# Convolution taps of the delta heads read PSUM accumulators: two bank pairs instead of padded SBUF rows

## The chip, the core and the metric

The kernel runs on one core of a Trainium2 chip. The metric is the device time of one execution in microseconds (us). The engines are written as the profile writes them: PE is TensorE's matrix multiplication and PEld its weight load, DVE is VectorE, ACT is ScalarE, POOL is GpSimd and SP is SyncE, which here issues the DMA transfers. Numbers such as L314 are lines of the kernel, as printed below.

## The reference, cut to what matters

Two blocks follow one another on a sequence of 1024 positions with 1024 features in float32. The first block projects the normalised input and has two kinds of heads: neighbourhood attention (8 heads of 64) and the gated delta rule (4 heads of 128). Before the delta rule, the projected q, k and v of the delta heads pass through a convolution of five taps, each channel by itself, centred, with zeros beyond both ends of the sequence, and then through SiLU:

```
def _centred_depthwise_conv(x, w):
    return lax.conv_general_dilated(x, w[:, None, :], window_strides=(1,),
        padding=[(DN_CONV // 2, DN_CONV // 2)],
        dimension_numbers=('NWC', 'WIO', 'NWC'), feature_group_count=c)
...
h = _rmsnorm(x, norm_w)
proj = jnp.einsum('bld,de->ble', h, w_in)
aq, ak, av, az, dq, dk, dv, dz, b_f, a_f, b_b, a_b = _split_proj(proj)
...
qkv = jax.nn.silu(_centred_depthwise_conv(jnp.concatenate([dq, dk, dv], axis=-1), conv_w))
dq, dk, dv = jnp.split(qkv, 3, axis=-1)
dq, dk, dv = _l2norm(to_bhld(dq)), _l2norm(to_bhld(dk)), to_bhld(dv)
...
o_f = _gated_delta_chunked(dq, dk, dv, g_f, beta_f)
o_b = flip(_gated_delta_chunked(flip(dq), flip(dk), flip(dv), flip(g_b), flip(beta_b)))
```

So there are 3 x 4 = 12 convolutions of a row block of 128 channels by 1024 positions. The gates (b, a) give decays between positions of a chunk, and each delta chunk needs a triangular solve. The second block (stick-breaking attention and retention) has a wider projection and takes most of the time; nothing in it is edited.

## The kernel before, in words

**Stages.** By the profile's clock the first block's preparation (load, norm, transposes into hT, the projection of the gates) lasts to about 57 us. The four delta heads follow, to about 230 us. Then come the projections of the neighbourhood attention (called na_proj here: products at L102 and L112, column blocks of 384 and 512), to about 302 us, while DVE and POOL still finish the last delta head. From there to about 460 us the neighbourhood attention (na) runs together with the triangular solver. The rest, to 2250 us, is the delta recurrence, the output projection and the second block. The delta rule's solver (L457 and L459, updates of X from the chunk matrices N in DRAM) works on all heads at once and so begins after the last head.

**Projection.** A product in float32 is made in three passes of a high and a low half (h1hi, h1lo with wu). Function dense_col makes one column block transposed, 128 channels by 1024 positions, as 48 matmuls of 128x512 at L112 into two PSUM accumulators; dense_tok makes 128 positions by n columns at L102. The weights come by DMA to raw, and POOL splits them into the halves (L70, L71) of wu.

**PSUM before.** There are two pools for the whole program: acc has three banks (each 128x512), z two, and t, o and p one each. They are never reopened.

**One delta head.** For each of q, k, v (index b): dense_col; two copies on ACT from the accumulators into a padded SBUF row pad of 1028 columns (L309), whose four edge columns POOL sets to zero (L306 and the line behind it); then on DVE the first tap as a product (L312) and four more taps that read pad shifted and add to cv (L314); then SiLU on ACT (L317). There are two buffers of pad and two of cv. From the results come rq (the norm of q, L324 and L325), the transposed and normalised k (kt, L335 to L340, through a z bank), kT (L349), v (vt), and for each direction the decays E (L379), the chunk matrices N (L400, from bank t), the matrices IT (L415, from bank p) and the scaled copies sct (L424, L428), which go to DRAM (d_N, d_pk, d_v). N and IT share two buffers with the tag IN; sct and vt share two.

**The gate chain.** Ahead of the heads, graw (the log decays) is summed along the positions by two matmuls (L279, L280) into a z bank, copied to gc (L281), transposed (L283), copied to growt (L285) and sent to DRAM (d_g).

**Order.** Each engine executes its instructions in a fixed order, which the framework's scheduler works out at build time from the dependencies and its own estimates. A pool's memory is reused only when everything that used it before has ended. So an edit of one place may move instructions of all engines around it.

## Time and profile before

| | before |
|---|---|
| median of 3 runs | 2250.59 us (2245.22 to 2253.38) |
| the profiled execution | 2252.17 us |
| its span, first to last instruction | 2250.5 us |
| mean granted TensorE clock | 0.984 |
| busy: PE, DVE, ACT, POOL | 2163.0, 1102.5, 766.0, 1105.4 us |

The profile is of one execution. Its time lies 1.6 us above the median and 1.7 us above its span. Busy times are those of whole instructions; a share of the clock of 1 is full speed. In a timeline a row has the start, the length, the engine, the line, the operation, output<-inputs, the shape and, in brackets, the idle time before it with what ended that idle time.

### The profile page before, as it was taken

Reading aid. Unit: us, or ns where it says so; the run is one execution under the profiler, and the core shown is the slowest. Engines: PE = TensorE matmul, PEld = TensorE weight load, DVE = VectorE, ACT = ScalarE, POOL = GpSimd, SP = SyncE. Lnnn points to the kernel's source line nnn. Section 1 sums busy time; section 2 is a strip of 40 time slices with the busy share of each in tenths; the row PEclk is TensorE's granted clock in tenths of the full one; section 3 lists DMA queues with packets and bytes.
Section 4 is the critical chain, followed back from the end, with each engine's and each line's share of the span. In section 5 each row is a group of like instructions: output and inputs, shape, how many; then the busy total and the mean of one; then the engine's idle time right before and its main releaser. Section 6 shows DMA issues by size and latency. Waiting matters only on the chain.

```text
span 2250.5 us, 33410 instructions
## 1 busy us (share of the span) xinstructions
PE 2163.0 (96%) x12325; PEld 1882.8 (84%) x12325; DVE 1102.5 (49%) x1980; ACT 766.0 (34%) x1912; POOL 1105.4 (49%) x1451
## 2 busy tenths in 40 slices
PE   7999888899999999999999999999999999999999
PEld 7777777787889878999999998888988888878887
DVE  4688879953446553566555655123333432231321
ACT  5354433445555322444333433112222322321200
POOL 6667777773101345344333334356565755354532
PEclk9999999899999999999999999999999999999999
DMA  4255740126377542111111112212333323564433
GB/s 132 83 152 157 206 129 26 36 82 190 90 278 246 176 130 63 41 61 57 57 42 34 43 57 71 89 58 79 107 94 120 126 92 114 179 227 159 146 109 106
DMA packets 240196, 250.27 MB, mean 111 GB/s; under 512 B 40161, under 2 KB 175521, under 8 KB 239777
## 3 DMA queue, kind: packets, MB, share of 16 engines
q1 hardware_dynamic: 240032, 248.14, 35.3%
q8 instruction: 97, 1.59, 0.3%
q14 instruction: 67, 0.54, 0.1%
HBM read 172.56 MB, written 75.53 MB: 110 GB/s over the span
## 4 chain that ended last, share of the span: by engine, by line
PE 68%; DVE 11%; POOL 6%; issue 5%; DMA 5%; ACT 2%; SPq 1%; POOLq 0%; DVEq 0%; ACTq 0%
PE acc L112 29%; PE acc L102 17%; PE acc L853 3%; PE po L1083 2%; PE pz L1051 2%; DVE X L459 2%; DVE svt L457 2%; POOL wu L71 2%; DVE cv L314 1%; POOL wu L70 1%; DMA raw<-in_w_in_dram 1%; PE pz L546 1%; PE pt L563 1%; POOL ss L126 1%; PE pp L577 1%
## 5 line engine op out<-in xcount | busy, mean ns | idle before, releaser
L112 PE MATMUL acc<-h2h,wu 128*128 128x512 f32 x1440 | 438.4, 393 | 0.7 <-ACT lg L958 0.7
L102 PE MATMUL acc<-wu,h2h 128*128 128x384 f32 (+1 forms) x1536 | 366.8, 322 | 6.6 <-ACT lg L972 2.2
L71 POOL TENSOR_TENSOR wu<-raw,wu 128x512 fp32r<-128x512 f32 (+3 forms) x276 | 366.3, 1335 | 7.2
L70 POOL TENSOR_SCALAR wu<-raw 128x512 fp32r<-128x512 f32 (+3 forms) x276 | 205.8, 749 | 313.0 <-PE acc L112 202.4
L112 PEld LDWEIGHTS acc<-h2h,wu 128*128 128x128 f32 x1440 | 269.5, 188 | 54.9 <-ACT lg L958 1.1
L102 PEld LDWEIGHTS acc<-wu,h2h 128*128 128x128 f32 x1536 | 265.8, 191 | 11.6 <-ACT lg L972 2.6
L112 PE MATMUL acc<-h2l,wu 128*128 128x512 f32 x720 | 265.2, 392 | 0.0
L102 PE MATMUL acc<-wu,h2l 128*128 128x384 f32 (+1 forms) x768 | 244.9, 321 | 0.0
L102 PE MATMUL acc<-wu,h1hi 128*128 128x384 f32 (+2 forms) x768 | 192.2, 334 | 11.1 <-DVE kS L512 5.2
L112 PE MATMUL acc<-h1hi,wu 128*128 128x512 f32 x512 | 167.3, 416 | 6.8 <-ACT pad L309 3.2
L125 POOL TENSOR_SCALAR ss<-ss 128x2 f32<-128x2 f32 (+2 forms) x136 | 36.7, 270 | 269.6 <-ACT sq L1001 215.0
L112 PEld LDWEIGHTS acc<-h2l,wu 128*128 128x128 f32 x720 | 135.0, 188 | 26.5
L102 PEld LDWEIGHTS acc<-wu,h1hi 128*128 128x128 f32 x768 | 137.0, 195 | 16.0 <-issue 6.5
L102 PEld LDWEIGHTS acc<-wu,h2l 128*128 128x128 f32 x768 | 146.1, 191 | 1.6
L112 PEld LDWEIGHTS acc<-h1hi,wu 128*128 128x128 f32 x512 | 100.4, 198 | 31.8 <-ACT pad L309 4.2
L102 PE MATMUL acc<-wu,h1lo 128*128 128x384 f32 (+2 forms) x384 | 126.7, 333 | 0.0
L126 POOL TENSOR_TENSOR ss<-ss,mhalf 128x2 f32<-128x2 f32 (+2 forms) x136 | 118.9, 875 | 8.3
L112 PE MATMUL acc<-h1lo,wu 128*128 128x512 f32 x256 | 97.9, 411 | 0.0
L1001 ACT ACTIVATE sq<-acc 128x128 f32<-128x128 f32 x128 | 35.5, 286 | 138.7 <-PE acc L102 125.8
L314 DVE SCALAR_TENSOR_TENSOR cv<-pad,c_conv_w,cv 128x1024 f32<-128x1024 f32 x48 | 76.6, 1596 | 1.1
L112 PE MATMUL acc<-oah,wu 128*128 128x512 f32 x256 | 76.1, 393 | 1.0 <-DVE sg L1275 0.6
L102 PEld LDWEIGHTS acc<-wu,h1lo 128*128 128x128 f32 x384 | 74.8, 195 | 0.4 <-issue 0.2
(553 smaller groups left out, 4438.1 us busy)
## 6 DMA issues: line engine op xcount, KB each, us to landing
raw<-in_w_in_dram SPq DMA_DIRECT2D x192, 256.0 KB, 3.0
d_pk<-sct SPq DMA_DIRECT2D x24, 512.0 KB, 4.3
raw<-in_w_out_dram SPq DMA_DIRECT2D x40, 256.0 KB, 3.0
wsa<-d_pk SPq DMA_DIRECT2D x16, 512.0 KB, 6.4
wsb<-d_pk SPq DMA_DIRECT2D x16, 512.0 KB, 7.4
d_sg<-lg SPq DMA_DIRECT2D x32, 256.0 KB, 2.4
sg<-d_sg SPq DMA_DIRECT2D x32, 256.0 KB, 3.4
raw<-in_w_in_dram SPq DMA_DIRECT2D x32, 192.0 KB, 2.8
```

Of the source, the lines that this page charges most:

```text
L70: nc.gpsimd.tensor_scalar(out=u[:, 0, :], in0=raw, scalar1=1.0, scalar2=0.0, op0=ALU.mult, op1=ALU.add)
L71: nc.gpsimd.tensor_tensor(out=u[:, 1, :], in0=raw, in1=f32(u[:, 0, :]), op=ALU.subtract)
L102: nc.tensor.matmul(acc[:, :n], lhsT=hT[a][:, k, m * P:(m + 1) * P], rhs=us[k][:, b, c0:c0 + n], start=(k == 0 and i == 0), stop=(k == NK - ...
L112: nc.tensor.matmul(accs[half], lhsT=us[k][:, b, c0:c0 + P], rhs=hT[a][:, k, half * 512:(half + 1) * 512], start=(k == 0 and i == 0), stop= ...
L125: nc.gpsimd.tensor_scalar(out=dst, in0=src, scalar1=mul, scalar2=eps, op0=ALU.mult, op1=ALU.add)
L126: nc.gpsimd.tensor_tensor(out=dst, in0=dst, in1=mhalf[:, :eshape], op=ALU.pow)
L314: nc.vector.scalar_tensor_tensor(out=cv, in0=pad[:, i:i + T], scalar=conv_w[:, blk, i:i + 1], in1=cv, op0=ALU.mult, op1=ALU.add)
L457: eng.tensor_tensor(out=tv, in0=X[:, a:a + n, j:j + 1].to_broadcast([P, n, w]), in1=X[:, j:j + 1, j + 1:64].to_broadcast([P, n, w]), op=AL ...
L459: eng.tensor_tensor(out=X[:, a:a + n, j + 1:64], in0=X[:, a:a + n, j + 1:64], in1=tv, op=ALU.add)
L853: nc.tensor.matmul(acc, lhsT=us[k][:, y, (b % 4) * P:(b % 4 + 1) * P], rhs=token_set(mT[x][:, k, 0:T], s), start=(k == 0 and i == 0), stop ...
L1051: nc.tensor.matmul(pz[:, :w], lhsT=qk[0][a][:, i * P:(i + 1) * P], rhs=qk[1][b][:, c0:c0 + w], start=(x == 0), stop=(x == 2))
L1083: nc.tensor.matmul(po[:, i0 * P:512], lhsT=v[a][:, c0 // P + kb, :], rhs=wT[b][:, :n], start=(diag and kb == 0 and x == 0), stop=(diag == ...
```

## The change

The PSUM pools are now opened and closed by a helper, banks(layout). Up to the heads and after them the layout is that of before (three accumulators a, two z banks, t, o, p). For the four delta heads it is two pairs c of two adjacent banks each, one z bank, t, o and p. All PSUM pools close and open at each switch. The projection of a delta block goes into a pair, so that its 1024 columns are contiguous. ACT makes the centre tap from the pair with a scale per channel and writes cv; DVE adds the four other taps, which read the pair shifted, over 1023 or 1022 columns, so that no padded row and no zeroed edges are needed. cv and sct (with vt) get three buffers instead of two, IN four instead of two.

```
-    psA = ctx.enter_context(tc.tile_pool(name="psA", bufs=3, space=PSUM))
-    psB = ctx.enter_context(tc.tile_pool(name="psB", bufs=1, space=PSUM))
+    def banks(layout):
+        while ps_pools:
+            ps_pools.pop().__exit__(None, None, None)
+        ps.clear()
+        for i, (tags, bufs) in enumerate(layout):
+            p_ = tc.tile_pool(name="ps" + tags, bufs=bufs, space=PSUM)
+            ps_pools.append(p_)
+            pl = p_.__enter__()
+            for t_ in tags:
+                ps[t_] = pl
+    banks((("a", 3), ("ztop", 1)))
...
+    banks((("c", 2), ("ztop", 1)))
     for h in range(4):
-        vt = dn.tile([P, NM, P], F32, tag="sct", name="vt", bufs=2)
+        vt = dn.tile([P, NM, P], F32, tag="sct", name="vt", bufs=3)
...
-            pad = dc.tile([P, T + 4], F32, tag="pad", name="pad", bufs=2)
-            nc.gpsimd.memset(pad[:, 0:2], 0.0)
-            nc.gpsimd.memset(pad[:, T + 2:T + 4], 0.0)
-            for half, acc in enumerate(dense_col(hT, us, b * P)):
-                nc.scalar.copy(out=pad[:, 2 + half * 512:2 + half * 512 + 512], in_=acc)
-            cv = dc.tile([P, T], F32, tag="cv", name="cv", bufs=2)
-            nc.vector.tensor_scalar_mul(out=cv, in0=pad[:, 0:T], scalar1=conv_w[:, blk, 0:1])
-            for i in range(1, 5):
-                nc.vector.scalar_tensor_tensor(out=cv, in0=pad[:, i:i + T], scalar=conv_w[:, blk, i:i + 1],
-                                               in1=cv, op0=ALU.mult, op1=ALU.add)
+            acc = pair()
+            dense_col(hT, us, b * P, acc)
+            cv = dc.tile([P, T], F32, tag="cv", name="cv", bufs=3)
+            for half in range(2):
+                hs = slice(half * 512, half * 512 + 512)
+                nc.scalar.activation(out=cv[:, hs], in_=acc[:, hs], func=AF.Copy, scale=conv_w[:, blk, 2:3])
+            for i in (1, 3, 0, 4):
+                a_, b_ = max(0, 2 - i), min(T, T + 2 - i)
+                nc.vector.scalar_tensor_tensor(out=cv[:, a_:b_], in0=acc[:, a_ + i - 2:b_ + i - 2], scalar=conv_w[:, blk, i:i + 1],
+                                               in1=cv[:, a_:b_], op0=ALU.mult, op1=ALU.add)
...
-                        N = dn.tile([P, 4, P], F32, tag="IN", name="N", bufs=2)
+                        N = dn.tile([P, 4, P], F32, tag="IN", name="N", bufs=4)
...
+    banks((("a", 3), ("ztop", 1)))
     naB = tc.tile_pool(name="naB", bufs=1, side="right")
```

In the changed kernel the lines lie 17 to 19 further down: L102 is L119, L112 is L129, L279 and L280 are L296 and L297, L283 is L300, the taps of L314 are L332, E of L379 is L397, N of L400 is L418, IT of L415 is L433, sct of L424 and L428 is L442 and L446. The order of all engines is the same again from about 635 us on.

**Where the heads begin.** PE before, from the last products ahead of the gate sums (L279, L280) on; those ahead are products of the first delta block, of which there are 37 ahead of the sums:

```order
L112 MATMUL acc<-h1lo_99,wu 128x512
L112 MATMUL acc<-h1hi_98,wu 128x512 x3
L112 MATMUL acc<-h1lo_99,wu 128x512 x2
L112 MATMUL acc<-h1hi_98,wu 128x512 x3
L279 MATMUL pz<-graw,trile 128x32
L280 MATMUL pz<-graw,trige 128x32
L112 MATMUL acc<-h1hi_98,wu 128x512
L112 MATMUL acc<-h1lo_99,wu 128x512 x2
L112 MATMUL acc<-h1hi_98,wu 128x512 x4
```

and in the changed kernel, where L119 is the projection of the gates, L296, L297 and L300 the gate chain, and L129 the first products into a pair:

```order
L119 MATMUL acc<-wu,h1lo_99 128x272
L119 MATMUL acc<-wu,h1hi_98 128x272 x2
L119 MATMUL acc<-wu,h1lo_99 128x272
L296 MATMUL pz<-graw,trile 128x32
L297 MATMUL pz<-graw,trige 128x32
L300 MATMUL pz<-ident,gc 64x128
L129 MATMUL pair<-h1hi_96,wu 128x512 x2
L129 MATMUL pair<-h1lo_97,wu 128x512 x2
```

The products of the first delta block stood ahead of the gate sums and now stand behind them and behind the transpose of gc.

**Where the heads end.** PE before: the last product of the twelfth delta block (L112) and the first products of na_proj (L102):

```order
L112 MATMUL acc<-h1hi_98,wu 128x512 x4
L112 MATMUL acc<-h1lo_99,wu 128x512 x2
L112 MATMUL acc<-h1hi_98,wu 128x512 x2
L102 MATMUL acc<-wu,h1hi_96 128x384 x2
L102 MATMUL acc<-wu,h1lo_97 128x384
L102 MATMUL acc<-wu,h1hi_96 128x384 x2
```

and in the changed kernel, with pair products (L129), the last head's chunk products (L414, L429), the sums for rq (L342), the transposes of k (L353), and then na_proj (L119):

```order
L129 MATMUL pair<-h1hi_98,wu 128x512 x4
L129 MATMUL pair<-h1lo_99,wu 128x512 x2
L129 MATMUL pair<-h1hi_98,wu 128x512 x2
L414 MATMUL pt<-kT 128x128 x4
L342 MATMUL pz<-ones_79,sq 128x2 x8
L353 MATMUL pz<-ident,s 128x128 x4
L429 MATMUL pp<-s,kT 128x128 x4
L119 MATMUL acc<-wu,h1hi_96 128x384 x2
L119 MATMUL acc<-wu,h1lo_97 128x384
L119 MATMUL acc<-wu,h1hi_96 128x384 x2
```

The first product of na_proj now writes a bank of a reopened pool, and waits in this order for the last tap of the twelfth convolution, which reads a pair in the same memory.

**The twelfth convolution on DVE.** Before, from its first tap (L312) to the last (L314), with IT (L415) and sct (L428) of the head before among them:

```order
L312 TENSOR_SCALAR cv<-pad,c_conv_w 128x1024
L415 TENSOR_TENSOR IT<-pp,E 128x512
L314 SCALAR_TENSOR_TENSOR cv<-pad,c_conv_w,cv 128x1024
L415 TENSOR_TENSOR IT<-pp,E 128x512
L314 SCALAR_TENSOR_TENSOR cv<-pad,c_conv_w,cv 128x1024 x2
L428 TENSOR_TENSOR sct<-kt,el 128x1024
L314 SCALAR_TENSOR_TENSOR cv<-pad,c_conv_w,cv 128x1024
L415 TENSOR_TENSOR IT<-pp,E 128x512
```

and in the changed kernel, its four taps at L332, with E (L397), rq (L343), el (L386, L391), sct (L442, L446) and IT (L433) among them:

```order
L332 SCALAR_TENSOR_TENSOR cv<-pair,c_conv_w,cv 128x1023
L397 TENSOR_TENSOR E<-G,gc 128x1024
L332 SCALAR_TENSOR_TENSOR cv<-pair,c_conv_w,cv 128x1023
L343 COPY rq<-pz 128x8
L386 TENSOR_TENSOR el<-G,gc 128x8
L442 TENSOR_TENSOR sct<-kT,G 128x1024
L446 TENSOR_TENSOR sct<-kt,el 128x1024
L332 SCALAR_TENSOR_TENSOR cv<-pair,c_conv_w,cv 128x1022
L433 TENSOR_TENSOR IT<-pp,E 128x512
L391 TENSOR_TENSOR el<-el,beta 128x8
L332 SCALAR_TENSOR_TENSOR cv<-pair,c_conv_w,cv 128x1022
```

Before, the five taps had two IT, one sct and one more IT behind; now the four taps have an E, two sct, one IT and small operations among them.

## Rows read from the trace of the kernel before

**Rows 1.** Stretches: length, busy PE, PEld, DVE, ACT, POOL, clock, DMA share, GB/s.

```profile
60.00:230.00 170.00, 159.28 (x759) 129.43 (x757) 137.47 (x121) 74.33 (x136) 117.25 (x109) 0.96 0.49 132
230.00:300.00 70.00, 57.14 (x308) 52.38 (x308) 50.25 (x75) 25.80 (x72) 49.48 (x50) 0.92 0.78 200
300.00:460.00 160.00, 142.23 (x836) 119.36 (x835) 150.03 (x331) 64.15 (x176) 128.48 (x182) 0.93 0.14 44
460.00:2250.00 1790.00, 1756.68 (x10126) 1538.34 (x10124) 740.06 (x1399) 568.23 (x1463) 772.38 (x1051) 0.99 0.34 111
```

**Rows 2.** Timeline of PE around the gate sums.

```profile
45.11 0.39 PE L112 MATMUL acc<-h1hi,wu 128*128 128x512 f32 x1
...
53.00 0.87 PE L112 MATMUL acc<-h1hi,wu 128*128 128x512 f32 x3
56.71 0.64 PE L279 MATMUL pz<-graw,trile 128*128 128x32 f32 x2 [2.84 <-DVE graw L275]
```

**Rows 3.** Timeline of DVE around the gate sums.

```profile
57.81 0.22 DVE L281 COPY gc<-pz 128x64 f32<-128x64 f32 x1 [1.16 <-PE pz L280]
65.08 0.28 DVE L285 COPY growt<-pz 64x128 f32<-64x128 f32 x1 [7.04 <-PE pz L283]
```

**Rows 4.** Busy time as in rows 1, of the stretch behind the gate sums.

```profile
55.00:65.00 10.00, 8.29 (x26) 6.70 (x27) 1.85 (x3) 0.00 (x0) 4.45 (x6) 0.66 0.57 164
```

**Rows 5.** Groups of DVE, 57 to 300 us: busy, mean ns | idle before, releasers.

```profile
L314 DVE SCALAR_TENSOR_TENSOR cv<-pad,c_conv_w,cv 128x1024 f32<-128x1024 f32 x48 | 76.6, 1596 | 1.1
L424 DVE TENSOR_TENSOR sct<-kT,G 128x1024 f32<-128x1024 f32 x8 | 14.3, 1785 | 4.3 <-POOL E L380 2.2 <-ACT kT L350 2.1
L428 DVE TENSOR_TENSOR sct<-kt,el 128x1024 f32<-128x1024 f32 x8 | 12.8, 1597 | 5.8 <-DMA d_pk<-sct 5.8
L312 DVE TENSOR_SCALAR cv<-pad,c_conv_w 128x1024 f32<-128x1024 f32 x12 | 11.7, 974 | 5.8 <-ACT pad L309 5.8
L379 DVE TENSOR_TENSOR E<-G,gc 128x1024 f32<-128x1024 f32 x8 | 11.4, 1423 | 0.0
L415 DVE TENSOR_TENSOR IT<-pp,E 128x512 f32<-128x512 f32 x16 | 10.7, 679 | 1.4 <-DMA d_pk<-IT 1.4
```

**Rows 6.** Lines L314, L400, L309: ns min/median/max; for L314 who waited (us, times).

```profile
L314 DVE SCALAR_TENSOR_TENSOR cv<-pad,c_conv_w,cv x48: 1269/1431/3252, 69.3 to 244.5; 128x1024 f32<-128x1024 f32 x48
...
  ACT s L317: 35.2, 8
  POOL pad L306: 12.7, 4
...
L400 DVE SCALAR_TENSOR_TENSOR N<-pt,E x16: 674/680/692, 117.2 to 275.2; 128x512 f32<-128x512 f32 x16
...
L309 ACT COPY pad<-acc x24: 566/588/596, 67.3 to 232.9; 128x512 f32<-128x512 f32 x24
```

**Rows 7.** Waits of PE, 40 to 300 us: total, times, longest.

```profile
PE po L349 <- DVE kt L340: 4.9, 4, 3.3
PE acc L508 <- DVE kn L500: 4.2, 3, 3.1
PE acc L112 <- ACT pad L309: 3.2, 3, 2.1
```

**Rows 8.** Timeline of PE at the end of the heads and of na_proj.

```profile
226.91 0.62 PE L112 MATMUL acc<-h1hi,wu 128*128 128x512 f32 x2
...
232.96 0.61 PE L102 MATMUL acc<-wu,h1hi 128*128 128x384 f32 x2 [2.79 <-ACT pad L309]
...
302.44 0.38 PE L531 MATMUL po<-ident,qd 128*128 128x128 f32 x2
```

**Rows 9.** Timeline of DVE: last tap, last N, first update of the solver.

```profile
244.46 1.62 DVE L314 SCALAR_TENSOR_TENSOR cv<-pad,c_conv_w,cv 128x1024 f32<-128x1024 f32 x1
...
274.35 1.50 DVE L400 SCALAR_TENSOR_TENSOR N<-pt,E 128x512 f32<-128x512 f32 x2
...
295.08 0.25 DVE L457 TENSOR_TENSOR svt<-X 128x54 f32<-128x54 f32 x1 [2.97 <-DMA X<-d_N]
```

More of the change, by code (lines that the diff above doesn't have):

```diff
@@ L47, in tile_kernel @@
     wpool = ctx.enter_context(tc.tile_pool(name="wpool", bufs=10))
-    psA = ctx.enter_context(tc.tile_pool(name="psA", bufs=3, space=PSUM))
-    psB = ctx.enter_context(tc.tile_pool(name="psB", bufs=1, space=PSUM))
+    ps = {}
+    ps_pools = []
+    def banks(layout):
[9 more added lines that the diff above has]
+    banks((("a", 3), ("ztop", 1)))
+    ctx.callback(banks, ())
     dram = ctx.enter_context(tc.tile_pool(name="dram", bufs=1, space=DRAM))
@@ L88, in bank, with pair @@
         if tag == "a":
-            return psA.tile([P, w], F32, tag="a", name="acc")
-        return psB.tile([P, w], F32, tag=tag, name="p" + tag, bufs=2 if tag == "z" else 1)
+            return ps["a"].tile([P, w], F32, tag="a", name="acc")
+        return ps[tag].tile([P, w], F32, tag=tag, name="p" + tag, bufs=2 if tag == "z" and "a" in ps else 1)
+    def pair():
+        return ps["c"].tile([P, T], F32, tag="c", name="pair")
     def dense_tok(hT, us, c0, n, order=None):
@@ L105, in dense_tok, with dense_col @@
                 yield m, a
-    def dense_col(hT, us, c0):
-        accs = [bank("a") for _ in range(2)]
+    def dense_col(hT, us, c0, acc2=None):
+        accs = [bank("a") for _ in range(2)] if acc2 is None else [acc2[:, 0:512], acc2[:, 512:1024]]
         for k in range(NK):
@@ L422, in tile_kernel @@
             for f, src in enumerate((kT, sT[0])):
-                sc_t = dn.tile([P, NM, P], F32, tag="sct", name="sct", bufs=2)
+                sc_t = dn.tile([P, NM, P], F32, tag="sct", name="sct", bufs=3)
                 (nc.gpsimd if f else nc.vector).tensor_tensor(out=sc_t.rearrange("p n c -> p (n c)"), in0=src, in1=G.rearrange("p n c -> p (n c)"),
@@ L426, in tile_kernel @@
                 nc.sync.dma_start(out=d_pk[d, :, :, f, h, :].rearrange("n p c -> p n c"), in_=sc_t)
-            sc_t = dn.tile([P, NM, P], F32, tag="sct", name="sct", bufs=2)
+            sc_t = dn.tile([P, NM, P], F32, tag="sct", name="sct", bufs=3)
             nc.vector.tensor_tensor(out=sc_t, in0=kt, in1=el[:, dh, :].unsqueeze(2).to_broadcast([P, NM, P]), op=ALU.mult)
```

4 lines of the change are left out of this document (2 added, 2 removed).

## The prediction

> **What bounds the kernel now.** The busy time in four stretches comes first [rows 1]. From 460 us on PE is busy for 1756.7 of 1790 us at a granted clock of 0.99. Nothing there is edited, so this stretch only moves as a whole. What the change can win or lose lies before 460 us. There PE sits idle for 170 - 159.3 = 10.7 us in the heads, 70 - 57.1 = 12.9 us in na_proj and 160 - 142.2 = 17.8 us in na. Where PE runs, its clock lies below full speed: (1 - clock) x length gives 6.8, 5.6 and 11.2 us. So about 65 us in all is not PE at its peak, and this is the pot.
>
> Next, who keeps PE waiting. DVE is busy for 137.5 of 170 us in the heads and for 150 of 160 us in na [rows 1]. PE's largest waits up to 300 us end with DVE's kt, DVE's kn and ACT's copies to pad [rows 7]. The copies in turn stand in ACT's queue behind SiLU, which waited 35.2 us in 8 cases for the last tap, and POOL waited 12.7 us to clear a pad [rows 6]. So in the heads PE and DVE are near each other, and DVE is what runs late: PE's last product of the twelfth delta block starts at 226.91 us [rows 8], and the last tap on it ends at 244.46 + 1.62 = 246.1 us [rows 9], 18.7 us behind the product's end at 227.4. At the far end the solver can't begin before the last N (274.35 us on) has gone to DRAM and come back as X: its first update is at 295.08 us [rows 9], 7 us before PE ends na_proj at 302.4 [rows 8]. From there DVE, with its 150 of 160 us, sets na.
>
> **The change, part by part.** The sum is made against the profiled execution, 2252.2 us; the median is 1.6 us lower.
>
> Opening switch. Before, 37 products of the first delta block ran from 45.11 us to 53.00 + 0.87 = 53.9 us, and the gate sums followed at 56.71 us, 2.84 us after them [rows 2]. These products gave PE work while ACT and DVE made graw. Now the pair pool opens only when all PSUM tiles of the preparation are done with, the last being the one that growt is copied from; the order shows all pair products behind the gate chain. That chain can't move forward, since graw doesn't. So the first pair product comes after the sums (56.71 + about 1.1), the copy of gc (57.81 + 0.22 [rows 3]), a transpose and the copy of growt (0.28 [rows 3]): about 59 us. 37 products of 8.8 / 37 = 0.237 us must be made up, 8.8 us, and PE reaches its 38th place some 1.4 us later by the chain: **+10**. The low clock behind the sums (0.66 [rows 4]) was there before and stays; bounds +8.8 to +14, the upper one if it lasts over those 37 too. What the earlier growt gives (65.08 before [rows 3], about 58.5 now) is that the decays E come early; DVE has nothing else then, so this counts in the next term.
>
> Heads. DVE loses 12 first taps of 0.974 us, 11.7 us [rows 5]. The other 48 took 1.596 us on average [rows 5], 1.269 at best and 3.252 at worst [rows 6]. No row shows a tap that reads PSUM over 1024 columns. The nearest is N, the same operation with one input in PSUM over 512 columns: 674 to 692 ns [rows 6], twice which is 1.36; the fastest tap from SBUF bounds it at 1.27. I take 1.30, as one long operation should lie under two short ones: 48 x 0.296 = 14.2 us. No gain at all is the other bound. So DVE has 25.9 us less of its 137.5. The centre tap on ACT takes the place of the copy (0.588 us [rows 6], 24 of both); even 0.1 us more each is hidden, since ACT is busy for 74 of 170 us [rows 1]. Were it not, 2.4 us is its whole cost. POOL's 24 clears and its wait of 12.7 us go; more buffers of sct and IN can take away DVE's waits of 5.8 and 1.4 us for DMA [rows 5]. A head then needs on DVE 12 x 1.30 (taps) + 3 x 1.42 (E) + 2 x 1.42 (E by beta, priced as E) + 10 x 0.68 (N, IT, kt) + 3.6 + 3.2 (sct) = 36 us and some small ones [rows 5, 6], about 38, where it was about 44; PE needs some 40: a quarter of the 182.3 us from 45.11 to 227.4 less 2.84, 10.7 and 6.8 of waits and low clock. PE becomes the slower of the two. Of its 10.7 idle and 6.8 clock I let 11.5 go: **-11.5**, bounds 0 and -17.5.
>
> Against it stands that less is held between product and taps. Before, two pads and the accumulators let PE end the product of block i+2 while the taps of block i ran; now block i+2 needs the pair of block i, free only after its fourth tap. Late taps up to one block's products (48 x 0.237 = 11.4 us) stay hidden, later ones stop PE. One z bank instead of two also puts the second half of k's transposes behind kt of the first.
>
> The Trainium skill ("Perfetto Trace Analysis", section Optimizing Scalar/DVE Operations) gives DVE about 60 ns of access overhead per instruction on SBUF and about 125 ns on PSUM. By that, as an estimate, 48 taps would save 3.1 us less, and the sum would be at most that much higher. No run here shows that difference by itself; N's rows contain whatever it is.
>
> Closing switch. Before, na_proj followed the last L112 product without a wait, and the first copy to pad stopped it later for 2.79 us [rows 8]. Now the order puts its first product behind the twelfth block's last tap. After PE's last pair product come on ACT two centre taps of 0.588 [rows 6], on DVE four taps of 1.30 with an E of 1.42, two sct of 1.79 and 1.60 and an IT of 0.68 between them [rows 5], and about 1 us of small ones and hand-overs: 13.3 us. Against that PE has 20 small products, some 2.5 us. So it idles 10.8 us, some 2.5 us go by the lower clock after it, and the old 2.79 us are gone: **+10.7**, bounds +8 (E and sct done sooner) and +20 (the old lag of 18.7 us and its clock).
>
> Rest of na_proj. DVE is some 7 us further there and na_proj's copies compete with less of the last head: I halve its 10.1 us of other idle time and 5.6 of clock: **-7.5**, bounds 0 and -15.7.
>
> Na. PE's last pair product should end near 226 us (227.4 + 10 - 11.5), so the last tap at 239 instead of 246. From there to the last N the order has two E, two E by beta, two kt, two IT, two sct and four N: 17 us [rows 5, 6], where it took 246.1 to 275.9. N is done about 16 us earlier, and X may start at about 279 us, while PE ends na_proj at 302.4 + 10 - 11.5 + 10.7 - 7.5 = 304. So DVE enters na with up to 18 us of solver behind it. But the order uses this: eight more updates stand ahead of the first reduction of na's scores, about 10 us. What stays is **-8**, bounds 0 and -19, of 29 us idle and clock there.
>
> Sum: +10 - 11.5 + 10.7 - 7.5 - 8 = -6.3 on 2252.2, 2245.9 us, and against the median **2244**.
>
> **Rivals.** (A) The sum as it stands: two new waits cost about what the faster heads and the earlier solver give. 2238 to 2253.
>
> (B) The early solver pays in full: DVE is busy for 150 of 160 us in na [rows 1], which speaks for it; the order, which puts updates ahead of the scores again, against. -19 instead of -8, and the closing at its lower bound: about 2230, 2224 to 2237.
>
> (C) The pair is held too long, slower. If E, sct and kt between the taps, with their own waits on POOL and ACT, keep the taps more than 11.4 us behind the products, PE stops at each pair. Speaking for it: DVE was 18.7 us late before; against: 38 us of DVE to 40 of PE per head. 2.5 us at each of the last nine pairs are 22 us: 2266, 2257 to 2275. It decides from about 2 us a pair on. The Trainium skill ("PSUM — Partial Sum Buffer", section Summary: rules for kernel authors) says to evacuate promptly because PSUM is tight; by that rule this case would come true. The trace of before shows banks evacuated by short copies and PE still waiting for them [rows 7], so it doesn't settle it.
>
> (D) The taps from PSUM take the 1.6 us of those from SBUF, so that only 11.7 of 25.9 us come: the heads give -5, closing costs 1.2 more, na gives -4: about 2256, 2250 to 2260. N's steady 0.68 speaks against it.
>
> **How the numbers follow.** A 0.42, B 0.25, C 0.20, D 0.13. A measurement of this kernel tells 0.5%, 11.3 us, from no change: below 2239.3 is faster, above 2261.8 slower. Faster is B and the edge of A, 0.31; slower most of C, 0.18; the rest 0.51. The range 2229 to 2264 leaves out the lower end of B (0.09) and the upper part of C (0.11). A's own range is 2238 to 2253.
>
> **What would show it.** Opening: PE without a product from about 45 to 59 us. Heads: L332 at 1.27 to 1.36 us, hardly spread; PE idle under 5 us from 65 us on, last pair product ending near 226 us. Closing: PE's wait ended by the last tap, 9 to 13 us. Last N near 260 us, the solver's first update near 279, na_proj's end near 304. The prediction is wrong if PE waits for taps within the heads (C), or if what stands at 460 us before comes more than 15 us earlier (B).

## The result, and the profile after

The changed kernel takes 2265.23 us (median of 5 runs, 2262.35 to 2266.81) against 2250.59 us for the kernel before in the same session. The ratio is 1.0078 [1.0062, 1.0093]: slower by 0.78%, 15 us by the medians, where no clear change was forecast, and 1 us above the range's upper end. The profiled execution has a span of 2265.1 us at a clock of 0.981.

The four stretches, as in [rows 1]:

```profile
60.00:230.00 170.00, 161.63 (x784) 132.83 (x784) 105.04 (x106) 69.13 (x131) 84.93 (x86) 0.98 0.49 132
230.00:300.00 70.00, 51.11 (x282) 48.91 (x282) 51.24 (x72) 29.80 (x75) 43.98 (x48) 0.82 0.84 220
300.00:460.00 160.00, 136.94 (x800) 115.82 (x799) 150.40 (x326) 59.75 (x159) 133.28 (x186) 0.93 0.13 41
460.00:2250.00 1790.00, 1758.60 (x10153) 1540.33 (x10154) 747.66 (x1405) 572.15 (x1477) 773.71 (x1050) 0.99 0.34 110
```

DVE's busy time in the heads fell from 137.5 to 105.0 us, and PE's idle time there from 10.7 to 8.4 us. What is worse lies behind: PE is idle for 18.9 us in na_proj's stretch, at a clock of 0.82, and for 23.1 us in na's.

PE at the opening, which answers to [rows 2] and [rows 3]:

```profile
57.65 0.61 PE L296 MATMUL pz<-graw,trile 128*128 128x32 f32 x2 [11.41 <-POOL wu L85]
58.07 0.61 PE L297 MATMUL pz<-graw,trige 128*128 128x32 f32 x2
59.00 0.42 PE L300 MATMUL pz<-ident,gc 128*64 128x128 f32 x1 [0.32 <-DVE gc L298]
59.89 1.19 PE L129 MATMUL pair<-h1hi,wu 128*128 128x512 f32 x2 [0.47 <-DVE growt L302]
```

PE stands from about 46 us (the gates' projection ends 1 us later than before) and begins with the first pair at 59.89 us, where "about 59" was forecast. (The row puts the 11.41 us down to POOL's wu; what the sums read is graw, which DVE ends at 57.55 us.)

The DVE groups, as in [rows 5], and who waited for the centre tap (L329) and for the taps (L332), as in [rows 6]:

```profile
L332 DVE SCALAR_TENSOR_TENSOR cv<-pair,c_conv_w,cv 128x1023 f32<-128x1023 f32 x24 | 30.7, 1280 | 22.5 <-ACT cv L329 22.2
L332 DVE SCALAR_TENSOR_TENSOR cv<-pair,c_conv_w,cv 128x1022 f32<-128x1022 f32 x24 | 30.6, 1276 | 0.3
```

```profile
L332 DVE SCALAR_TENSOR_TENSOR cv<-pair,c_conv_w,cv x48: 1265/1282/1285, 74.0 to 248.1; 128x1023 f32<-128x1023 f32 x24, 128x1022 f32<-128x1022 f32 x24
...
  ACT cv L329: 22.2, 7
...
  ACT s L335: 26.8, 7
...
L329 ACT ACTIVATE cv<-pair,c_conv_w x24: 670/685/707, 72.7 to 232.3; 128x512 f32<-128x512 f32 x24
```

A tap from PSUM takes 1.265 to 1.285 us, with hardly a spread. DVE sat idle for 22.2 us, in 7 cases, until ACT had made the centre tap. But 17.9 us of these lie in the first four convolutions, where ACT itself waits for PE's product and makes the centre tap at once; DVE only keeps PE's pace there. The second convolution, on ACT and on DVE:

```profile
83.86 1.27 ACT L329 ACTIVATE cv<-pair,c_conv_w 128x512 f32<-128x512 f32 x2 [2.17 <-PE pair L129]
```

```profile
85.16 5.24 DVE L332 SCALAR_TENSOR_TENSOR cv<-pair,c_conv_w,cv 128x1023 f32<-128x1023 f32 x4 [5.90 <-ACT cv L329]
```

PE and DVE at the end of the heads and of na_proj, which answer to [rows 8] and [rows 9]:

```profile
228.59 0.64 PE L129 MATMUL pair<-h1hi,wu 128*128 128x512 f32 x2
...
233.95 3.57 PE L342 MATMUL pz<-ones,sq 128*128 128x2 f32 x16 [3.84 <-ACT sq L339]
238.49 1.11 PE L353 MATMUL pz<-ident,s 128*128 128x128 f32 x4 [0.96 <-DVE rq L343]
248.15 2.08 PE L429 MATMUL pp<-s,kT 128*128 128x128 f32 x8 [8.55 <-DVE IT L433]
249.88 0.99 PE L119 MATMUL acc<-wu,h1hi 128*128 128x384 f32 x2
```

```profile
248.09 1.27 DVE L332 SCALAR_TENSOR_TENSOR cv<-pair,c_conv_w,cv 128x1022 f32<-128x1022 f32 x1
...
271.57 1.27 DVE L418 SCALAR_TENSOR_TENSOR N<-pt,E 128x512 f32<-128x512 f32 x2
...
292.06 0.25 DVE L476 TENSOR_TENSOR svt<-X 128x54 f32<-128x54 f32 x1 [7.38 <-DMA X<-d_N]
```

The last pair product ends at 229.2 us, 1.7 us later than before. The last tap ends at 249.4 us, 20.2 us behind the product, and 0.5 us later comes na_proj's first product, at 249.88 instead of 227.37. (The profile puts PE's wait of 8.55 us down to IT, since the chunk products L429 stand ahead of na_proj in the queue and needed the bank that IT read; the last tap ended 1.3 us later still.) With na_proj's and na's products of L102 and L119 matched by their count, the lateness is 17.8 us at 253, 8.3 us at 270, 10.9 us at 307, 14.3 us at 447 and 14.6 us at the end. The last N ends at 272.8 us and the solver starts at 292.06, 3 us earlier than before [rows 9], where 16 were forecast.

### The profile page after: what moved, and what is told of

The parts are those of the page before. It is cut to its first block, busy times and chain, and to the rows that moved or that the text cites. A ratio compares the mean times of both kernels' runs of the same rounds, so it can differ in the third digit from the quotient of the medians.

```text
span 2265.1 us, 33370 instructions
## 1 busy us (share of the span) xinstructions
PE 2157.4 (95%) x12325; PEld 1882.7 (83%) x12325; DVE 1081.9 (48%) x1968; ACT 765.7 (34%) x1910; POOL 1073.3 (47%) x1427
## 4 chain that ended last, share of the span: by engine, by line
PE 70%; DVE 9%; POOL 7%; issue 5%; DMA 5%; ACT 2%; SPq 0%; POOLq 0%; ACTq 0%; DVEq 0%
PE acc L129 29%; PE acc L119 17%; PE pair L129 3%; PE acc L872 3%; PE po L1102 2%; PE pz L1070 2%; DVE X L478 2%; POOL wu L85 2%; DVE svt L476 2%; POOL wu L84 1%; DMA raw<-in_w_in_dram 1%; PE pz L565 1%; POOL ss L143 1%; PE pt L1223 1%; PE pt L1097 1%
## 5 line engine op out<-in xcount | busy, mean ns | idle before, releaser
L129 PE MATMUL acc<-h2h,wu 128*128 128x512 f32 x1440 | 438.1, 392 | 0.4 <-ACT lg L977 0.4
L119 PE MATMUL acc<-wu,h2h 128*128 128x384 f32 (+1 forms) x1536 | 366.6, 322 | 6.4 <-DVE sq L1026 2.0
L85 POOL TENSOR_TENSOR wu<-raw,wu 128x512 fp32r<-128x512 f32 (+3 forms) x276 | 352.4, 1285 | 8.5
L84 POOL TENSOR_SCALAR wu<-raw 128x512 fp32r<-128x512 f32 (+3 forms) x276 | 193.5, 703 | 328.4 <-PE acc L129 191.1
L129 PEld LDWEIGHTS acc<-h2h,wu 128*128 128x128 f32 x1440 | 269.3, 188 | 54.9 <-ACT lg L977 0.8
L119 PEld LDWEIGHTS acc<-wu,h2h 128*128 128x128 f32 x1536 | 265.8, 190 | 11.4 <-issue 2.3
L129 PE MATMUL acc<-h2l,wu 128*128 128x512 f32 x720 | 265.0, 392 | 0.0
L119 PE MATMUL acc<-wu,h2l 128*128 128x384 f32 (+1 forms) x768 | 244.8, 320 | 0.0
L119 PE MATMUL acc<-wu,h1hi 128*128 128x384 f32 (+2 forms) x768 | 194.5, 336 | 7.7 <-DVE kS L531 7.1
L129 PEld LDWEIGHTS acc<-h2l,wu 128*128 128x128 f32 x720 | 134.8, 188 | 26.5
L119 PEld LDWEIGHTS acc<-wu,h1hi 128*128 128x128 f32 x768 | 138.6, 197 | 11.8 <-issue 8.7
L119 PEld LDWEIGHTS acc<-wu,h2l 128*128 128x128 f32 x768 | 145.9, 190 | 1.6
L119 PE MATMUL acc<-wu,h1lo 128*128 128x384 f32 (+2 forms) x384 | 127.2, 334 | 0.0
L129 PE MATMUL pair<-h1hi,wu 128*128 128x512 f32 x384 | 109.5, 402 | 1.2 <-DVE cv L332 0.8
L129 PEld LDWEIGHTS pair<-h1hi,wu 128*128 128x128 f32 x384 | 72.1, 191 | 17.8 <-DVE cv L332 1.2
L129 PE MATMUL acc<-oah,wu 128*128 128x512 f32 x256 | 75.8, 392 | 0.3 <-POOL wu L84 0.3
L119 PEld LDWEIGHTS acc<-wu,h1lo 128*128 128x128 f32 x384 | 75.0, 196 | 0.4 <-issue 0.2
L129 PE MATMUL acc<-obh,wu 128*128 128x512 f32 x256 | 74.9, 389 | 0.0
L1102 PE MATMUL po<-wT,v 128*128 128x512 f32 (+3 forms) x288 | 74.0, 351 | 0.4
```

What stands on the lines that cost most here:

```text
L84: nc.gpsimd.tensor_scalar(out=u[:, 0, :], in0=raw, scalar1=1.0, scalar2=0.0, op0=ALU.mult, op1=ALU.add)
L85: nc.gpsimd.tensor_tensor(out=u[:, 1, :], in0=raw, in1=f32(u[:, 0, :]), op=ALU.subtract)
L119: nc.tensor.matmul(acc[:, :n], lhsT=hT[a][:, k, m * P:(m + 1) * P], rhs=us[k][:, b, c0:c0 + n], start=(k == 0 and i == 0), stop=(k == NK - ...
L129: nc.tensor.matmul(accs[half], lhsT=us[k][:, b, c0:c0 + P], rhs=hT[a][:, k, half * 512:(half + 1) * 512], start=(k == 0 and i == 0), stop= ...
L1102: nc.tensor.matmul(po[:, i0 * P:512], lhsT=v[a][:, c0 // P + kb, :], rhs=wT[b][:, :n], start=(diag and kb == 0 and x == 0), stop=(diag == ...
```

## The experiments

Each is given as its ratio to the kernel before, from 5 rounds on the same chip; the changed kernel stands at 1.0078. The kernel before had medians of 2246.8 to 2250.6 us in the sessions, so 0.001 is 2.25 us. Every edit also moves the scheduler's order of all engines, so that 0.1 or 0.2% need not be the edit's own doing.

### The two switches of the banks

Opening eased: z, t, o and p are in a pool that stays, the gate sums use its z, and only the three accumulators and a second z bank (y) are given up for the pairs.

```
-    banks((("a", 3), ("ztop", 1)))
+    fixed = ctx.enter_context(tc.tile_pool(name="psztop", bufs=1, space=PSUM))
+    banks((("a", 3), ("y", 1)))
...
-    banks((("c", 2), ("ztop", 1)))
+    banks((("c", 2),))
```

> The changed kernel with only the opening switch eased: z, t, o and p stay open throughout, the gate sums use the z bank that stays, and only the three accumulators and the second z bank give way to the pairs. In the order 35 pair products stand ahead of the gate sums again. Theory 1, the loss sits in the two switches (opening about 11 us, closing about 20 us gross): PE has products from about 46 us on, the heads' products end near 219 us, and the time falls by 8 to 11 us, to 2254 to 2257. Theory 2, the switches only shift idle time, since the neighbourhood attention is set by DVE and swallows what PE gains before it, and the loss comes from the other order there: 2261 to 2266.

Measured: 1.0023 [1.0012, 1.0034], 0.55% or 12 us less than the change, a little more than theory 1 had. The first pair product starts at 46.27 us. But the third block, which needs the first pair, then has to wait for taps, and the heads end at 223.4 us, not 219:

```profile
46.27 0.70 PE L138 MATMUL pair<-h1hi,wu 128*128 128x512 f32 x2 [0.76 <-ACT dzt L267]
...
75.94 1.13 PE L138 MATMUL pair<-h1hi,wu 128*128 128x512 f32 x2 [3.50 <-DVE cv L341]
```

Closing eased: the two pairs lie in pools of their own, c and d, each at one end of PSUM (side closes the pool at an end and opens another there), so that na_proj's first accumulators take the pair of the eleventh convolution.

```
-    banks((("c", 2), ("ztop", 1)))
+    side("right", "c", 1)
+    side("left", "d", 1)
...
-    banks((("a", 3), ("ztop", 1)))
+    side("right", "a", 2)
+    side("left", "by", 1)
```

> The changed kernel with only the closing switch eased: the two pairs lie in pools of their own, so that the first two accumulators of na_proj take the pair of the eleventh convolution and do not wait for the twelfth. The gate sums are put into the accumulators, so that the opening still waits for the gate chain. Theory 1 (the two switches): PE goes on with na_proj within 2 us of the last pair product near 230 us, where it now starts at 249.9 us; the time falls by 8 to 14 us, to 2251 to 2257. Theory 2 (the attention swallows it, its order costs): 2261 to 2266.

Measured: 1.0059 [1.0045, 1.0073], 4 us less. na_proj does follow the last pair product at once (229.84 us), and at 447 us the kernel is only 3 us behind the one before instead of 14. Its profiled execution ends 14 us behind the one before. More than half of the 11 us between is lost at 540 to 560 us, where the clock is 0.50, the lower of its two levels, 1.2 instead of 2.4 GHz (mean before: 0.83), so that these 20 us are worth 6.6 us less:

```profile
229.84 0.60 PE L137 MATMUL acc<-wu,h1hi 128*128 128x384 f32 x2
...
520.00:540.00 20.00, 15.52 (x114) 11.33 (x112) 8.29 (x36) 14.49 (x31) 4.90 (x5) 0.96 0.73 265
540.00:560.00 20.00, 18.24 (x111) 14.05 (x111) 4.67 (x14) 9.40 (x21) 2.88 (x2) 0.50 0.30 83
```

Both switches eased:

> The changed kernel with both switches eased. Theory 1 (the two switches): the two gains add, 2265 less 18 to 24 us, so 2241 to 2247, below the kernel before, since the heads keep their gain of about 10 us. Theory 2 (the attention swallows it, its order costs): 2258 to 2265, above the kernel before.

Measured: 1.0024 [1.0012, 1.0036]. Nothing is added to the opening alone. Both theories failed in part: the switches cost, but not as a sum.

The gate chain's small pool kept until the heads end, on top of both:

```
-    gp_ = tc.tile_pool(name="gp", bufs=1)
+    gp_ = tc.tile_pool(name="gp", bufs=1, side="right")
...
-    gp_.__exit__(None, None, None)
...
     dn_.__exit__(None, None, None)
+    gp_.__exit__(None, None, None)
```

> The changed kernel with both switches eased, and the small pool of the gate chain kept open until the heads end, so that the first cv no longer takes its memory and need not wait for growt to be in DRAM. With both switches eased, PE waited 6.9 us for the first convolution's taps, since the third block needs the first pair. Theory 1, two pairs hold less between product and tap than the two pads and the accumulators did, and that wait is the price of it: the wait falls under 2 us, the heads end 4 to 7 us earlier, and the time falls by 3 to 7 us against the kernel with both switches eased, to 0.998 to 1.001 of the kernel before. Theory 2, PE's gain in the heads is swallowed later, since the last tap and the last N stay where they are: no more than 2 us, 1.001 to 1.003.

Measured: 1.0007 [0.9993, 1.0021], a time of theory 1, but not its way: the wait for the first taps fell only from 6.9 to 5.2 us and the heads end 1 us earlier, not 4 to 7. The intervals of this and the former overlap.

The new banks with the old convolution (and its old numbers of buffers):

```
-            acc = pair()
-            dense_col(hT, us, b * P, acc)
...
+            for half, acc in enumerate(dense_col(hT, us, b * P, pair())):
+                nc.scalar.copy(out=pad[:, 2 + half * 512:2 + half * 512 + 512], in_=acc)
```

> The banks of the change with the convolution of before: product into a pair, two ACT copies to a padded row, five taps from SBUF on DVE, two buffers each as before. The pair is free after the copies, and the order lets na_proj follow the last product directly, so that only the opening switch and the single z bank remain. Theory 1 (the two switches): the opening's 11 us stay, the heads gain nothing, and PE does not wait at the end: before plus 9 to 13 us, 2260 to 2264, with taps of 1.6 us. Theory 2 (attention's order): the time follows the order there and not the switches, so it could as well lie at before's 2250. If the taps from PSUM are themselves harmful to PE (pair held long), this kernel must be clearly faster than the changed one, under 2258.

Measured: 1.0036 [1.0024, 1.0048], some 8 us over the kernel before (2256.6 us, under the 2258 named): near the opening's 10, a little under theory 1's 9 to 13, and 9 us less than the changed kernel. The closing waits for no tap here (PE stands 3.35 us ahead of na_proj for something that the trace does not name) and is worth 4 of the 9 by the run above. The other 5 lie with the new convolution, although it takes 32 us off DVE in the heads, or with the larger buffers, which this kernel lacks and which cost 5 us by themselves (next run). So the banks are not the whole loss.

### Buffers and the solver's place

In the kernel before:

```
-        vt = dn.tile([P, NM, P], F32, tag="sct", name="vt", bufs=2)
+        vt = dn.tile([P, NM, P], F32, tag="sct", name="vt", bufs=3)
...
-                        N = dn.tile([P, 4, P], F32, tag="IN", name="N", bufs=2)
+                        N = dn.tile([P, 4, P], F32, tag="IN", name="N", bufs=4)
```

> The kernel before with only the larger buffers: three of sct and vt, four of IN; banks and convolution as before. Theory 1, the buffers are worth the 7 us that DVE waited for DMA of sct and IT, but DVE had slack later: within 4 us of the kernel before. Theory 2, the larger buffers change the order (the solver's updates further ahead of the scores) and are what costs in the attention: 5 us or more slower than the kernel before.

Measured: 1.0023 [1.0010, 1.0036], 5 us slower, so theory 2's size, at its lower end. But not its way: 12 of the solver's updates stand ahead of the first reduction of na's scores on DVE, where the kernel before has 13. PE's waits for the weights that POOL splits grew in the heads:

```profile
PE acc L112 <- POOL wu L71: 5.7, 4, 2.2
```

where the kernel before has 3.1 us in 2 waits. The last product of the heads ends 3.3 us later, at 230.9 us, so most of the loss lies in the heads, and the buffers gave nothing by themselves.

In the changed kernel, the solver's place:

```
-            take(sol, 4)
+            take(sol, 3)
```

> The changed kernel with the solver's steps taken three instead of four at each step of the attention, which moves its updates back among the scores. Theory 1, what the change loses at its two switches it keeps: the time stays at 2263 to 2268. Theory 2, the solver's updates ahead of the scores cost in the attention: 4 to 10 us faster, 2255 to 2261.

Measured: 1.0086 [1.0066, 1.0106], no gain. But the edit did not move the solver: by the traces DVE's order differs from that of the changed kernel in two swaps of neighbours near 425 us and PE's in one, and in both kernels 20 updates stand ahead of the first reduction of scores, where the kernel before has 13. So this run tests neither theory, and what the solver's place costs stays open.

### The centre tap

The centre tap on DVE:

```
-            for half in range(2):
-                hs = slice(half * 512, half * 512 + 512)
-                nc.scalar.activation(out=cv[:, hs], in_=acc[:, hs], func=AF.Copy, scale=conv_w[:, blk, 2:3])
+            nc.vector.tensor_scalar_mul(out=cv, in0=acc, scalar1=conv_w[:, blk, 2:3])
```

> The changed kernel with the centre tap on DVE in place of ACT: one product over 1024 columns from the pair, so five DVE operations per convolution. DVE gets about 12 x 1.25 = 15 us more, of the 65 us that it is now idle from 60 to 230 us. Theory 1, DVE's saving does not reach PE because each convolution passes from ACT to DVE and back, and DVE stood idle 22 us for ACT's centre taps: the last tap comes within 16 us of the last pair product (now 20.2), and the time falls by 2 to 6 us, to 2259 to 2263. Theory 2, DVE's work itself is what makes the last tap late (the decays, sct and IT between the taps): the last tap comes later by 1 to 4 us and the time rises to 2265 to 2269.

Measured: 1.0010 [0.9998, 1.0021]. This one edit, which gives DVE 15.4 us more work, takes away 15 us, more than either theory had. The heads' products end at 222.7 us and the last tap at 238.0.

ACT's order alone: the centre tap stays on ACT, and SiLU of q and k is made to stand behind the next block's centre taps.

```
+                tap = nc.scalar.activation(out=cv[:, hs], in_=acc[:, hs], func=AF.Copy, scale=conv_w[:, blk, 2:3])
+            while late:
+                s_, cv_ = late.pop(0)
+                si = nc.scalar.activation(out=s_, in_=cv_, func=AF.Silu)
+                tc.add_manual_dep(si.ins, tap.ins.name, NOSYNC, reason="order")
...
-            nc.scalar.activation(out=s, in_=cv, func=AF.Silu)
+            late.append((s, cv))
```

> The changed kernel with the centre tap on ACT as in the change, but ACT's order altered: SiLU of q stands behind k's centre taps and SiLU of k behind v's, so that no centre tap of k or v waits behind a SiLU that waits for taps on DVE. Nothing else is edited. Theory 1, the loss comes from ACT's queue (a centre tap behind a waiting SiLU, and DVE's taps behind it): at least half of the 15 us that the centre tap on DVE gave comes back, 1.001 to 1.004 of the kernel before. Theory 2, it is the passing from ACT to DVE as such, or ACT's reading of the pair, whatever the order: 1.006 to 1.009.

Measured: 1.0006 [0.9995, 1.0016], 16 us less than the change, with the same operations on the same engines, and more than theory 1 had. DVE still waits for the centre tap (L331), about as long as in the change:

```profile
  ACT cv L331: 18.4, 7
```

What is gone are PE's waits within the heads. In the changed kernel they are 8.2 us from the first pair product to the last, most of them for SiLU, whose s PE transposes:

```profile
PE pt L363 <- ACT s L335: 5.3, 2, 3.6
```

With ACT's order altered they are 0.4 us. PE and DVE at the end of the heads:

```profile
219.39 0.63 PE L130 MATMUL pair<-h1hi,wu 128*128 128x512 f32 x2
223.43 2.77 PE L351 MATMUL pz<-ones,sq 128*128 128x2 f32 x16 [3.42 <-ACT sq L348]
237.41 2.04 PE L438 MATMUL pp<-s,kT 128*128 128x128 f32 x8 [11.20 <-DVE IT L442]
239.10 0.99 PE L120 MATMUL acc<-wu,h1hi 128*128 128x384 f32 x2
```

```profile
237.18 1.27 DVE L338 SCALAR_TENSOR_TENSOR cv<-pair,c_conv_w,cv 128x1022 f32<-128x1022 f32 x1
...
263.65 1.29 DVE L427 SCALAR_TENSOR_TENSOR N<-pt,E 128x512 f32<-128x512 f32 x2 [0.45 <-PE pt L423]
...
283.99 0.24 DVE L485 TENSOR_TENSOR svt<-X 128x54 f32<-128x54 f32 x1 [8.14 <-DMA X<-d_N]
```

The last pair product ends at 220.0 us instead of 229.2, the last tap at 238.45 instead of 249.36, and the solver starts 8 us earlier. The closing is hardly better: na_proj begins 19.1 us behind the last pair product's end, where it was 20.7.

ACT still reads the pair, DVE doesn't wait for it (in the kernel with the centre tap on DVE):

```
+            spare = dc.tile([P, T], F32, tag="spare", name="spare", bufs=2)
+            for half in range(2):
+                hs = slice(half * 512, half * 512 + 512)
+                nc.scalar.activation(out=spare[:, hs], in_=acc[:, hs], func=AF.Copy, scale=conv_w[:, blk, 2:3])
```

> The changed kernel with the centre tap on DVE, and ACT still multiplying the pair by the centre weight, into a tile that nobody reads (extra work, 24 operations of 0.69 us on ACT). ACT has the load of the change and holds each pair as the change does; only DVE no longer waits for ACT. Theory 1, the loss is DVE's wait for ACT: 1.000 to 1.003, near the centre tap on DVE alone (1.001). Theory 2, the loss is ACT's load, or pairs that come free late: 1.005 to 1.009.

Measured: 1.0034 [1.0022, 1.0046], between the theories. About 5 us of the loss come back with ACT's load and the pairs that it holds (or the order that follows from them); the other 10 are gone when DVE's taps no longer build on what ACT wrote.

One more product on DVE, likewise:

```
+            nc.vector.tensor_scalar_mul(out=spare, in0=acc, scalar1=conv_w[:, blk, 2:3])
```

> The changed kernel with the centre tap on DVE and one more product of the same size on DVE per convolution, into a tile that nobody reads: 12 x 1.28 = 15.4 us more on DVE in the heads. Theory 1, in the heads DVE has slack and its throughput no longer sets the time: within 4 us of the centre tap on DVE alone, 1.000 to 1.003. Theory 2, DVE's time in the heads reaches the end one to one: 10 to 16 us more, 1.0055 to 1.008.

Measured: 1.0026 [1.0012, 1.0040], 3.6 us more than without, which is theory 1's size. The two intervals overlap: a microsecond of DVE added in the heads cost about a quarter of one at the end, and anything from nothing to a half fits.

### Together

The edits above in combination, first the centre tap on DVE with the opening eased, with the closing, with both, and with both and the gate chain's pool:

> The changed kernel with the centre tap on DVE and the opening switch eased. With the centre tap on ACT the eased opening was worth 0.55% of the time. Theory 1, the centre tap on DVE and the opening are separate losses: another 6 to 12 us on top of the centre tap on DVE alone (which stood at 1.001 of the kernel before), 0.996 to 0.998. Theory 2, from the neighbourhood attention on DVE sets the pace (about 150 of 160 us busy in every variant), and what comes before it only counts once: 0.999 to 1.002.

> The changed kernel with the centre tap on DVE and the closing switch eased, the opening as in the change. PE still waited at the closing for some 9 us with the centre tap on DVE (3.4, 3.1 and 2.4 us). Theory 1 (separate losses): 3 to 6 us less than with the centre tap on DVE alone, 0.998 to 1.000. Theory 2 (the attention swallows it): 1.000 to 1.002.

> The changed kernel with the centre tap on DVE and both switches eased. Theory 1 (separate losses): 10 to 15 us under the centre tap on DVE alone, 0.994 to 0.997, faster than the kernel before. Theory 2 (the attention swallows it): 0.999 to 1.002.

> As the kernel with the centre tap on DVE and both switches eased, with the gate chain's pool kept open until the heads end, so that the first cv doesn't wait for growt. With the centre tap on ACT this was worth 0.17%, within the intervals. Theory 1 (separate losses): 0 to 4 us under the former, 0.992 to 0.997. Theory 2 (the attention swallows it): 0.999 to 1.002.

Measured: 0.9982 [0.9972, 0.9993], 1.0010 [0.9995, 1.0026], 0.9991 [0.9973, 1.0009] and 0.9985 [0.9973, 0.9996]. The first and the last beat the kernel before, by 4 and 3 us. The opening gave 6 us, the closing nothing, and none of the four reached the gain that theory 1 had for it, though the first came to 0.0002 of it.

Then ACT's order with the opening eased, and with both and the gate chain's pool:

> The changed kernel with ACT's order altered (SiLU behind the next centre taps) and the opening switch eased. ACT's order alone stands at 1.0006 of the kernel before; the eased opening was worth 0.55% with ACT's old order and 0.28% with the centre tap on DVE. Theory 1, opening and ACT's queue are separate losses of the heads: 0.995 to 0.998, faster than the kernel before. Theory 2, once the heads end early the attention, in which DVE is busy 150 of 160 us, takes the rest: 0.999 to 1.001.

> The changed kernel with ACT's order altered, both switches eased, and the gate chain's pool kept open until the heads end. Theory 1 (separate losses): below the kernel with ACT's order and the opening alone, 0.993 to 0.997. Theory 2 (the attention takes the rest, and with it the closing): no faster than that one, 0.997 to 1.001.

Measured: 1.0023 [1.0010, 1.0036] and 0.9990 [0.9974, 1.0005]. Here the opening by itself gave nothing, and neither theory has this time: the heads' products end at 217.1 us, 3 us earlier than with ACT's order alone, but the solver starts no earlier, at 284.8 us. With the closing and the gate chain's pool eased as well the time falls by 0.33%, clear of both intervals. Theory 2 of the last kernel had excluded that, though its time is the one that came.

## Why the prediction was wrong

**The step that failed** is this one: "The centre tap on ACT takes the place of the copy (0.588 us [rows 6], 24 of both); even 0.1 us more each is hidden, since ACT is busy for 74 of 170 us [rows 1]. Were it not, 2.4 us is its whole cost." The duration was as assumed (0.69 us instead of 0.59). But the cover was taken from ACT's busy share, and what counts is what stands ahead of the instruction in ACT's queue. In the first six convolutions the second half of the centre tap begins 0.6 to 1.3 us behind the product's end, but in the last six 5.3, 2.5, 0.6, 9.3, 6.5 and 3.1 us behind it; with ACT's order altered these are 5.4, 0.6, 0.6, 3.6, 2.8 and 0.6. (DVE's wait of 22.2 us for the centre tap is no measure of this, since 18.4 us of it stay with the altered order.) ACT's queue in the changed kernel, around the tenth convolution:

```profile
182.22 1.06 ACT L339 ACTIVATE sq<-s 128x1024 f32<-128x1024 f32 x1
183.30 1.28 ACT L385 ACT_TABLE_LOAD   x1
197.66 0.22 ACT L385 ACTIVATE eS<-G 128x8 f32<-128x8 f32 x1 [13.07 <-DMA G<-d_g]
...
201.08 1.06 ACT L335 ACTIVATE s<-cv 128x1024 f32<-128x1024 f32 x1
...
203.56 1.25 ACT L329 ACTIVATE cv<-pair,c_conv_w 128x512 f32<-128x512 f32 x2
```

and DVE's and PE's in the same stretch:

```profile
190.97 1.27 DVE L332 SCALAR_TENSOR_TENSOR cv<-pair,c_conv_w,cv 128x1022 f32<-128x1022 f32 x1
197.66 0.17 DVE L386 TENSOR_TENSOR el<-G,gc 128x8 f32<-128x8 f32 x1 [5.42 <-DMA G<-d_g]
...
204.84 1.28 DVE L332 SCALAR_TENSOR_TENSOR cv<-pair,c_conv_w,cv 128x1023 f32<-128x1023 f32 x1 [0.80 <-ACT cv L329]
```

```profile
202.19 0.67 PE L363 MATMUL pt<-ident,s 128*128 128x128 f32 x4 [3.62 <-ACT s L335]
```

ACT stands for 13.07 us at eS, the exponential of the last column of G (the third head's decays), until G has come from DRAM; behind it stand two more exponentials, the SiLU of the ninth convolution and then the centre taps of the tenth at 203.56. PE stands 3.62 us for that same SiLU. DVE ends the taps of the ninth at 192.2 and begins those of the tenth at 204.84, but it stands 5.42 us of this for G itself. With ACT's order altered the centre taps of the tenth begin at 194.6 us instead of 203.6, eS waits 2.78 us instead of 13.07, PE's waits within the heads are 0.4 us instead of 8.2, and the heads end 9.2 us earlier. Which of the entries costs most, SiLU behind taps or eS behind G, the runs don't separate: the altered order changed both.

It is not the only step that failed. The lateness against the kernel before, by stage, with the products of PE matched by their count and the end taken from the spans of the profiled executions:

| stage, up to | forecast | changed kernel | ACT's order altered |
|---|---|---|---|
| opening and heads, the last product of the twelfth block | -1.5 | +1.7 | -7.5 |
| closing, 253 us | +10.7 | +16.1 | +12.6 |
| na_proj, 307 us | -7.5 | -6.9 | -6.7 |
| na and what follows, the end | -8 | +3.7 | -0.9 |
| sum | -6.3 | +14.6 | -2.5 |

Of the 21 us between forecast and measurement, 3 came in the heads, 5 in the closing, less than 1 in na_proj and 12 behind 307 us.

**Opening**, +10: right as it was worked out (first pair product at 59.89 us; easing it took 12 us from the changed kernel, though only 6 with the centre tap on DVE and nothing with ACT's order altered). **The taps**, 1.30 us: right (1.28), and rival D with it is out. **Heads**, -11.5: from the first product to the last the changed kernel needs 169.3 us against 178.7 before (45.1 to 227.5 us, by 226.91 + 0.62, where the prediction has 227.4; less the 3.7 us from 53.9 to 57.6), -9.4; with ACT's order altered 160.2, -18.5. **Closing**, +10.7: mis-sized by its own list. The last tap came 20.2 us behind the product, not 13.3; with ACT's order altered it is still 18.4 us. DVE's rows behind the product's end at 229.2 us show what the list lacks: two sct, two N and an IT of the last head ahead of the first tap (to 233.8 us), a wait for G, and longer E (2.21 us instead of 1.42) and sct (3.36 instead of 1.60):

```profile
229.29 1.22 DVE L442 TENSOR_TENSOR sct<-kT,G 128x1024 f32<-128x1024 f32 x1
...
234.96 2.21 DVE L397 TENSOR_TENSOR E<-G,gc 128x1024 f32<-128x1024 f32 x1
...
240.37 0.80 DVE L386 TENSOR_TENSOR el<-G,gc 128x8 f32<-128x8 f32 x1 [1.94 <-DMA G<-d_g]
...
242.95 3.36 DVE L446 TENSOR_TENSOR sct<-kt,el 128x1024 f32<-128x1024 f32 x1
```

That the last tap comes at 238.45 us with ACT's order altered, where 239 was forecast, is luck: the heads end 6 us earlier there than forecast, and the lag is 5 us longer. **Solver**: forecast at 279, 292.06 in the change and 283.99 with the altered order; from the last tap to the last N it took 23 us in the change, not 17.

**Na**, -8: this is the larger miss, and it failed by itself. The step took the solver's early start to pull na forward, and the runs do not bear that out. A mark for na is the 32nd reduction of its scores on DVE, the last of the two passes that run beside the solver. In the kernel before, with ACT's order altered, and with the switches and the gate chain's pool eased on top of that:

```profile
515.98 0.69 DVE L554 CUSTOM_DVE_ANT_0 s<-pz,tb 128x512 f32<-128x512 f32 x1
```

```profile
513.18 0.69 DVE L582 CUSTOM_DVE_ANT_0 s<-pz,tb 128x512 f32<-128x512 f32 x1
```

```profile
502.21 0.69 DVE L603 CUSTOM_DVE_ANT_0 s<-pz,tb 128x512 f32<-128x512 f32 x1
```

In the second kernel the solver starts 11.1 us earlier than before and na gains 2.8; in the third it starts 8.4 us earlier and na gains 13.8. What differs is na_proj, whose first product comes at 239.1 us in the second and at 218.9 in the third. In the 14 runs whose products of na_proj match those of before one to one, the mark lies within 4.5 us of the lateness that PE has at 300 us (-3.5 to +11.1), while the solver starts 12 us earlier to 9 us later. So na goes with PE's projections and not with the solver's start, and where the closing holds these up, it takes what the heads gain. (Each run changes the order in more than one place, so this is a reading of all of them together.) Why the lateness still grows by 3.7 us behind 307 us in the change, perhaps by the 20 updates ahead of the first scores, stays open.

Nor does na swallow every gain, though DVE is busy for 150 of 160 us there. Where both the closing is eased and the centre tap is on DVE or ACT's order altered, the mark comes 9 to 14 us earlier than before, and the heads end 5 to 10 us earlier. Part of this is lost behind it: in the profiled execution with the centre tap on DVE and both switches eased (2255.8 us, where the median is 2243.8) the clock from 520 to 580 us is 0.64, 0.68 and 0.91, against 1.00, 0.83 and 1.00 before, which is 12 us at full speed.

**Rival C**'s time came, by another way: PE waited 0.8 us for a pair in the changed kernel, so the pairs were not what stopped it. In the eight kernels with the opening eased the third block did wait, 3.5 to 7.2 us, which is the smaller store between product and taps that the prediction named. The Trainium skill's rule to evacuate PSUM promptly ("PSUM — Partial Sum Buffer", section Summary: rules for kernel authors) is not borne out by the 0.8 us of the changed kernel; the waits with the opening eased agree with it.

## What to carry to other kernels

An operation moved to a half-idle engine is hidden only if nothing that waits stands ahead of it in that engine's queue; read the waits of the instructions ahead, not the busy share. A wait that the profile puts down to an engine need not be that engine's doing: most of the 22.2 us for ACT's centre tap was PE's own pace, and stayed when the loss was gone. A stage that begins only behind the last reader of the one before can lose there what the one before has gained. And an edit of the program's text need not change the order on the engines: read the order before the time.
